# Sums over the normed rows ahead of the shift, the table load tied to the last SiLU, and the modulation tiles moved out of layer 0's last W_down piece

## The chip, the cores and the metric

The kernel runs on one core of one Trainium2 chip. Its time is device microseconds for one execution of the whole program. The chip has a matrix engine (TensorE, PE in the profile), a vector engine (VectorE, DVE), a scalar engine (ScalarE, ACT), GpSimd (POOL) and a queue engine that issues the transfers (SyncE, SP). Each engine works its own list of instructions in order.

## The reference

Two layers of a hybrid decoder on 512 rows of 1024 numbers, all in f32. Cut to what matters here:

```
c_act = silu(c)
for l in range(2):
    mod = c_act @ w_ada[l] + b_ada[l]                      # 6 x 1024 numbers
    sh1, sc1, g1, sh2, sc2, g2 = split(mod, 6)
    h = rmsnorm(x, norm1_w[l]) * (1 + sc1) + sh1
    x = x + g1 * hybrid_mixer(h)                           # W_in, attention, SSD, W_out
    h = rmsnorm(x, norm2_w[l]) * (1 + sc2) + sh2
    g, u = split(h @ w_gate_up[l], 2)                      # 1024 -> 2 x 2816
    x = x + g2 * ((silu(g) * u) @ w_down[l])               # 2816 -> 1024
```

## The kernel before

Activations lie transposed: `xT` holds 8 tiles (k = 0 to 7) of 128 features by 512 rows. Each f32 matmul operand is split into a rounded part and the rest (`hh` and `hl` for the normed rows, `hi`/`lo` for weights), and a product is three matmuls: hi with hi, hi with lo, lo with hi. ScalarE makes the rounded part (a CAST or an ACTIVATE), VectorE the rest. H0 and H1 are the two halves of 256 rows.

The **norm** (`Norm`): ScalarE squares, GpSimd adds up (`acc`; the last one on VectorE), TensorE sums over partitions (`nst`), ScalarE takes Ln and then Exp of it (`na`), VectorE finishes the reciprocal root in PSUM (`nst`). `hid` then makes, for each k, `ht` (x times gain times root, VectorE), `hh` (ScalarE, with the shift `sh` as its bias) and `hl` (VectorE).

The **FFN** (`ffn`) takes the 22 gate and up tiles one after the other. Tiles 0, 1 and each odd one are plain products; each even tile f from 2 on is done by seven smaller products (`product`), for which sums and differences of the four quarters of h (`b11`, `b12`, `b21`, `b22`, here called the block sums) are split into `t1` to `t4` at the head of the FFN, and sums of weight quarters (`sf`, `sh`, `sl`) are made per tile. W_down runs in three pieces (after tiles 5, 13 and 21); a piece loads its 8 weight tiles as `rawd`, splits them into `hid` and `lod`, and `add` puts each of the 8 outputs `dps` into `xT`. In the third piece the last three outputs are done half by half (`dps05a`, `06a`, `07a`, then `05b`, `06b`, `07b`).

The **modulation** `mod` of layer 1 is made during layer 0: `ada_some(n)` takes n of the 40 queued tiles (128x1024, `rawa`), each one transfer of 512 KB and one VectorE instruction. `rawa`, `rawd` and the weights of the mixer (`raw`, `rawr`) share three buffers of the tag `raw`, in turn.

**ScalarE's tables.** Silu needs one table set, Ln and Exp another that holds both. `exp_ln_tables()` (L249) loads that one by hand; where the active table lacks a function, the build puts a load of its own (shown at L155) before the instruction. The last FFN piece calls `exp_ln_tables()` after its last tile, and the scheduler may place it among the SiLUs in front of it:

```
if c1 == FT:
    exp_ln_tables()
```

PE's order is pinned to the program's order in the FFN; the order of ScalarE, VectorE and SP is chosen by a scheduler from its own costs when the program is built. In layer 1's mixer, `rows` makes `rps` from slabs of W_in (`hir`, and `lor` on GpSimd), then `wps` tiles of the rest are interleaved with the latents' up-projections `kvps` and `qps`, their norms (`yk`, `yy`) and transposes (`tk`, `tq`).

Of the kernel before, what the change touches and what calls it, by code (L numbers as in the profile page):

```python
# [8 lines left out]
F32 = mybir.dt.float32  # L9
# [3 lines left out]
AF = mybir.ActivationFunctionType  # L13
ALU = mybir.AluOpType
# [58 lines left out]
P = 128  # L73
S = 512
D = 1024
KT = D // P
# [9 lines left out]
FT = DFF // P  # L86
# [107 lines left out]
def trunk(ctx, tc, xin, cin, pos, eye, consts, small, wada, ws, out):  # L194
    nc = tc.nc
    ve, se, ge = Kept(tc, nc.vector), Kept(tc, nc.scalar), nc.gpsimd
# [4 lines left out]
    tp = ctx.enter_context(tc.tile_pool(name="tp", bufs=3))  # L201
# [3 lines left out]
    def T(name, shape=None, dt=F32, tag="t", pool=tp, **k):  # L205
        return pool.tile(shape or [P, S], dt, name=name, tag=tag, **k)
# [41 lines left out]
    def exp_ln_tables():  # L248
        tc.keep_in_program_order(nc.scalar.preload_act_table_set("natural_log_exp_and_others"))  # L249
# [78 lines left out]
    mods = [cp.tile([P, 48], F32, name=f"mods{l}") for l in range(L)]  # L328
# [27 lines left out]
    def ada_some(n, pool=None, pin=None):  # L356
        for _ in range(n):
            if ada_q:
                l, t = ada_q.pop(0)
                raw = None  # L360
                if pool is not None:
                    raw = pool.tile([P, 8, P], F32, name=f"rawa{l}_{t}", tag="rawa", bufs=2)
                ada1(l, t, raw, pin)
                if t % 8 == 7:
                    ada_fin(l, t - 7, t + 1)
# [51 lines left out]
            for k in ks:  # L417
                hid(self.l, self.which, h, k, rb, sl, **kw)

    def hid(l, which, h, k, rb, sl=slice(0, S), eng=None, full=None, pool=tp):  # L420
        o = 0 if which == 1 else 8
        so = (0 if which == 1 else 24) + k
        sh = mods[l][:, so:so + 1]
        hh, hl = h
        n = sl.stop - sl.start
        t = T(f"ht{l}{which}{k}_{sl.start}", [P, n] if pool is not tp else None, pool=pool, **({"bufs": 4} if pool is not tp else {}))
        ve.scalar_tensor_tensor(t[:, :n], xT[:, k, sl], gn[l][:, o + k:o + k + 1], rb[:, :n], op0=ALU.mult, op1=ALU.mult)
        if full is not None:
            se.activation(full, t[:, :n], AF.Identity, bias=sh)
        if hh is None:  # L430
            return
        se.activation(hh[:, k, sl], t[:, :n], AF.Identity, bias=sh)
        if eng is not None:
            u = T(f"hu{l}{which}{k}_{sl.start}")[:, :n]
            se.activation(u, t[:, :n], AF.Identity, bias=sh)
            return eng.tensor_tensor(hl[:, k, sl], u, hh[:, k, sl].bitcast(F32), op=ALU.subtract)
        return ve.scalar_tensor_tensor(hl[:, k, sl], t[:, :n], sh, hh[:, k, sl].bitcast(F32), op0=ALU.add, op1=ALU.subtract)

    hid_hl = (cp.tile([P, KT, S], F32R, name="hh"), cp.tile([P, KT, S], F32R, name="hl"))
# [567 lines left out]
    def ffn(l, mix, nrm2, kept):  # L1007
# [7 lines left out]
        H0, H1 = HALVES  # L1015
        HW = S // 2
        K4 = KT // 2
        hh, hl = hid_hl
# [4 lines left out]
        with tc.tile_pool(name=f"ff{l}", bufs=1) as fp:  # L1023
# [3 lines left out]
            raw, rd, sta, sf, px, py, pz, sg, p5, w, whole, gps = ({} for _ in range(12))  # L1027
# [16 lines left out]
            def tile_weights(f, i):  # L1044
                whole[f, i] = weights(raw[f][i], f"{'uw'[i]}{l}_{f}")
# [55 lines left out]
            def c12(f):  # L1101
                se.copy(sg[f][:, H1], pz[f])
                ve.tensor_tensor(sg[f][:, H1], sg[f][:, H1], px[f], op=ALU.add)
                se.activation(sg[f], sg[f], AF.Silu)

            def c22(f):
                ve.tensor_tensor(p5[f], p5[f], px[f], op=ALU.add)
# [12 lines left out]

            def gate_silu(f):
                sg[f] = T(f"sg{l}{f}")
                se.activation(sg[f], gps[0], AF.Silu)


            hp = ExitStack()
            hpool = hp.enter_context(tc.tile_pool(name=f"hf{l}", bufs=1))
            (b11, b12), (b21, b22) = ([hpool.tile([P, K4, HW], F32, name=f"b{i}{j}{l}") for j in (1, 2)] for i in (1, 2))
            full = lambda k, half: ((b11, b12), (b21, b22))[k // K4][half][:, k % K4, :]
            rb = None  # L1130
            for i, _ in enumerate(out_proj(l, mix, nrm2, H1, kept)):
                if i % KT == KT - 1:
                    i //= KT
                    if i == 0:
                        rb = nrm2.scale(H0)
                    else:
                        for k in (i - 1, i) if i == KT - 1 else (i - 1,):
                            nrm2.apply(hid_hl, rb, H0, (k,), full=full(k, 0))
                    if i in (3, 5):
                        loads(i // 2 - 1)  # L1140
                    if i >= KT - 2:
                        tile_weights(0, i - KT + 2)
# [10 lines left out]
            half(H0, range(K4))  # L1153
            rb2 = nrm2.scale(H1, tag="my")
            half(H0, range(K4, KT))
            for k in range(KT):
                nrm2.apply(hid_hl, rb2, H1, (k,), full=full(k, 1), pool=hpool)
            half(H1, range(KT))
            tile_weights(1, 0)
            ve.tensor_tensor(b11, b12, b11, op=ALU.subtract)  # L1160
            split(*ts[1], b11)
            tile_weights(1, 1)
            ve.tensor_tensor(b12, b22, b12, op=ALU.subtract)
            ve.tensor_tensor(b22, b22, b11, op=ALU.subtract)
            split(*ts[2], b22)
            ve.tensor_tensor(b21, b21, b22, op=ALU.subtract)
            split(*ts[3], b12)
            split(*ts[4], b21)
            hp.close()
# [1 line left out]
            with tc.tile_pool(name=f"ac{l}", bufs=1) as ap:  # L1171
# [5 lines left out]
                for pc, (c0, c1) in enumerate(PIECES):  # L1177
# [39 lines left out]
                    for f in range(c0, c1):  # L1217
                        if f == 0:
                            gate_silu(0)
                            unit(0, gps[1])  # L1220
                            loads(2)
                            ada_some(1)
                        elif f not in FAST and f - 1 not in FAST:
                            loads(f + 2)
                            tile_half(f, 0)
                            gate_silu(f)
                            tile_half(f, 1)
                            unit(f, gps[1])
                            sums(f + 1)
                            loads(f + 3)  # L1230
                            ada_some(1)
                        elif f in FAST:
                            g = f + 1
                            product(1, f)
                            product(2, f)
                            c11(f)
                            if late is not None:
                                product(4, late)
                                unit(late)
                            product(5, f)  # L1240
                            copy5(f)
                            tile_weights(g, 0)
                            tile_half(g, 0)
                            gate_silu(g)
                            product(6, f)
                            product(3, f)
                            c12(f)
                            tile_weights(g, 1)
                            loads(g + 2)
                            if g < c1 - 1:  # L1250
                                sums_a(g + 1)
                            else:
                                fetch(0)
                                fetch(1)
                                fetch(2)
                            tile_half(g, 1)
                            unit(g, gps[1])
                            product(7, f)
                            c22(f)
                            if g < c1 - 1:  # L1260
                                sums_b(g + 1)
                                loads(g + 3)
                            else:
                                ready(0)
                                ready(1)
                            late = f
                            if c0 == 0:
                                ada_some(3)
                    if c1 == FT:
                        exp_ln_tables()  # L1270
                    ps = {m: bank("mm", f"dps{l}{pc}_{m}") for m in (0, 1)}
                    slow = [f - c0 for f in (late, c1 - 1)]
                    ks = [k for k in range(n) if k not in slow]
# [12 lines left out]
                    for m in range(last):  # L1286
                        fetch(m + 3)
                        if m > 0:
                            ready(m + 2)
                        if m > 1:  # L1290
                            ps[m] = bank("mm", f"dps{l}{pc}_{m}")
                            down(m, FULL, range(n), ps[m])
                        add(ps[m], m, FULL)
                        ada_some(2)
                    if c1 == FT:
                        ready(KT - 1)
                tail = range(last, KT)
# [20 lines left out]
    h = None  # L1318
# [194 lines left out]
```

## Time and profile before

| | |
|---|---|
| median of 3 runs | 1312.83 us (1312.13 to 1312.91) |
| profiled execution | 1313.35 us, its span 1311.6 us |
| TensorE | 1206.6 us busy, 92% of the span; mean granted clock 0.967 |
| VectorE | 881.5 us, 67% |
| ScalarE | 625.8 us, 48% |
| GpSimd | 239.9 us, 18% |
| chain that ended last | PE 62%, DVE 16%, DMA 7%, ACT 7% |

The span is one execution from its first to its last instruction. A row of waits names the waiting engine with what it writes and its line, the releaser behind the arrow, then the total in us, how many waits, and the longest. A row of the timeline has the start, the duration in us, engine, line, operation, out and in, and in brackets the idle time ahead of it. Layer 0's FFN is at 297 to 683 us, layer 1's mixer from there to 925 us, layer 1's FFN to the end.

### The profile page before, as it was taken

Reading aid. Unit: us, or ns where it says so; the run is one execution under the profiler, and the core shown is the slowest. Engines: PE = TensorE matmul, PEld = TensorE weight load, DVE = VectorE, ACT = ScalarE, POOL = GpSimd, SP = SyncE. Lnnn points to the kernel's source line nnn. Section 1 sums busy time; section 2 is a strip of 40 time slices with the busy share of each in tenths; the row PEclk is TensorE's granted clock in tenths of the full one; section 3 lists DMA queues with packets and bytes.
Section 4 is the critical chain, followed back from the end, with each engine's and each line's share of the span. In section 5 each row is a group of like instructions: output and inputs, shape, how many; then the busy total and the mean of one; then the engine's idle time right before and its main releaser. Section 6 shows DMA issues by size and latency. Waiting matters only on the chain.

```text
span 1311.6 us, 18321 instructions
## 1 busy us (share of the span) xinstructions
PE 1206.6 (92%) x7076; PEld 1035.9 (79%) x7076; DVE 881.5 (67%) x1517; ACT 625.8 (48%) x1064; POOL 239.9 (18%) x177
## 2 busy tenths in 40 slices
PE   7879797788999999999977789988989999999998
PEld 6668674688887998899867677757978899889988
DVE  6979778879858755864565675475898456445532
ACT  4356764437532442244335977754664244324430
POOL 2651154352000000000152220446300000000000
PEclk8899998898999999999998999989999999999999
DMA  8433344463428533841343211212626343233021
GB/s 313 157 121 119 107 145 126 137 218 109 157 89 271 194 113 112 282 141 30 117 143 89 63 51 64 65 48 60 201 98 210 109 128 90 71 120 110 29 79 66
DMA packets 48727, 162.45 MB, mean 124 GB/s; under 512 B 5440, under 2 KB 8832, under 8 KB 48640
## 3 DMA queue, kind: packets, MB, share of 16 engines
q1 hardware_dynamic: 48640, 161.29, 38.6%
q8 instruction: 55, 0.90, 0.3%
q14 instruction: 32, 0.26, 0.1%
HBM read 159.14 MB, written 2.13 MB: 123 GB/s over the span
## 4 chain that ended last, share of the span: by engine, by line
PE 62%; DVE 16%; DMA 7%; ACT 7%; issue 4%; POOL 3%; DVEq 0%; ACTq 0%; POOLq 0%; SPq 0%
PE gup L139 19%; PE dps L139 11%; PE gx L139 9%; PE ops L139 5%; PE gz L139 4%; PE wps L139 4%; DMA rawa<-wada 3%; DVE rawa L155 2%; PE sc L139 2%; PE gy L139 2%; DMA raw<-ws 2%; DMA rawd<-ws 1%; PE pt L142 1%; ACT L155 1%; DVE qr L155 1%
## 5 line engine op out<-in xcount | busy, mean ns | idle before, releaser
L155 ACT CAST hid<-rawd 128x1024 fp32r<-128x1024 f32 (+1 forms) x48 | 46.6, 978 | 174.2 <-PE dps L139 62.9
L139 PE MATMUL dps<-ah,hid 128*128 128x512 f32 x304 | 120.5, 396 | 0.5 <-ACT hid L155 0.5
L139 PE MATMUL dps<-ah,lod 128*128 128x512 f32 x304 | 120.3, 396 | 0.5 <-DVE lod L155 0.5
L139 PE MATMUL dps<-al,hid 128*128 128x512 f32 x304 | 120.2, 395 | 0.0
L399 POOL TENSOR_TENSOR acc<-acc,sq 128x256 f32<-128x256 f32 x36 | 44.2, 1231 | 382.0 <-ACT sq L155 381.9
L155 DVE SCALAR_TENSOR_TENSOR rawa<-rawa,cb 128x1024 f32<-128x1024 f32 x77 | 100.9, 1320 | 11.7 <-DMA rawa<-wada 11.3
L155 ACT CAST hiu<-rawg 128x1024 fp32r<-128x1024 f32 x44 | 46.0, 1048 | 98.1 <-PE gup L139 53.6
L155 DVE TENSOR_TENSOR lou<-rawg,hiu 128x1024 fp32r<-128x1024 f32 x44 | 53.7, 1221 | 51.5 <-ACT hiu L155 51.3
L139 PE MATMUL gup<-hh,hiu 128*128 128x512 f32 (+1 forms) x208 | 79.0, 380 | 6.7 <-ACT hh L155 6.7
L155 DVE SCALAR_TENSOR_TENSOR xT<-dps,mods,xT 128x512 f32<-128x512 f32 x42 | 31.4, 749 | 71.9 <-PE dps L139 71.8
L139 PE MATMUL gup<-hh,lou 128*128 128x512 f32 (+1 forms) x208 | 78.7, 378 | 1.0 <-DVE lou L155 1.0
L139 PE MATMUL gup<-hl,hiu 128*128 128x512 f32 (+1 forms) x208 | 79.0, 380 | 0.3 <-DVE hl L155 0.2
L139 PE MATMUL gup<-hh,hiw 128*128 128x512 f32 (+1 forms) x208 | 79.0, 380 | 0.0
L139 PE MATMUL ops<-hh,hi 128*128 128x256 f32 x256 | 75.3, 294 | 3.9 <-DVE xT L155 1.7
L139 PE MATMUL gup<-hh,low 128*128 128x512 f32 (+1 forms) x208 | 78.7, 379 | 0.0
L139 PE MATMUL gup<-hl,hiw 128*128 128x512 f32 (+1 forms) x208 | 78.4, 377 | 0.0
L155 DVE TENSOR_TENSOR lod<-rawd,hid 128x1024 fp32r<-128x1024 f32 (+1 forms) x48 | 54.2, 1133 | 35.1 <-ACT hid L155 34.5
L139 PE MATMUL ops<-hl,hi 128*128 128x256 f32 x256 | 73.1, 286 | 1.0 <-POOL hl L443 1.0
L139 PE MATMUL ops<-hh,lo 128*128 128x256 f32 x256 | 73.1, 286 | 0.8 <-POOL lo L291 0.8
L139 PE MATMUL wps<-hh,hi 128*128 128x512 f32 x168 | 70.7, 421 | 2.4 <-DVE xbc L155 2.4
L139 PEld LDWEIGHTS dps<-ah,lod 128*128 128x128 f32 x304 | 57.1, 188 | 15.2 <-DVE lod L155 1.4
L139 PEld LDWEIGHTS dps<-ah,hid 128*128 128x128 f32 x304 | 57.1, 188 | 14.4 <-ACT hid L155 1.3
(438 smaller groups left out, 3696.9 us busy)
## 6 DMA issues: line engine op xcount, KB each, us to landing
rawg<-ws SPq DMA_DIRECT2D x88, 512.0 KB, 3.8
rawa<-wada SPq DMA_DIRECT2D x80, 512.0 KB, 4.3
raw<-ws SPq DMA_DIRECT2D x49, 512.0 KB, 3.7
rawd<-ws SPq DMA_DIRECT2D x32, 512.0 KB, 3.7
raws<-wada SPq DMA_DIRECT2D x16, 512.0 KB, 5.0
rawd<-ws SPq DMA_DIRECT2D x16, 384.0 KB, 3.6
ar<-ard SPq DMA_DIRECT2D x8, 512.0 KB, 3.9
rawk<-ws SPq DMA_DIRECT2D x8, 404.0 KB, 5.4
```

The source lines that it names most:

```text
L139: self._put(self.tc.nc.tensor.matmul(out, lhsT, rhs, **kw), 4 * n if rhs.dtype == F32 else n)
L142: self._put(self.tc.nc.tensor.transpose(out, in_, eye), 0.116)
L155: i = f(*args, **kw)
L399: (ve if last else eng or ge).tensor_tensor(self.acc[:, sl], self.acc[:, sl], sq, op=ALU.add)
```

## The change

It has three parts, all in `ffn` and `hid`.

1. The block sums are taken from `ht`, the rows before the shift. `hid` no longer writes an f32 copy of the shifted rows on ScalarE; `ht` is written straight into the tile `tt`, and the shift enters the sums through `sh` or `dsh` (a difference of shifts) as a per-partition scalar. Three of the four sums of 128x1024 become four instructions of 128x256 each.
2. `exp_ln_tables()` in the last piece waits for the last two SiLUs.
3. In the second and third piece `ada_some(1)` is called after each even tile, and `ada_some(2)` no longer in the W_down part of the third piece.

```
-    def hid(l, which, h, k, rb, sl=slice(0, S), eng=None, full=None, pool=tp):
+    def hid(l, which, h, k, rb, sl=slice(0, S), eng=None, full=None):
...
-        t = T(f"ht{l}{which}{k}_{sl.start}", [P, n] if pool is not tp else None, pool=pool, **({"bufs": 4} if pool is not tp else {}))
+        t = T(f"ht{l}{which}{k}_{sl.start}") if full is None else full[:, k, sl]
         ve.scalar_tensor_tensor(t[:, :n], xT[:, k, sl], gn[l][:, o + k:o + k + 1], rb[:, :n], op0=ALU.mult, op1=ALU.mult)
-        if full is not None:
-            se.activation(full, t[:, :n], AF.Identity, bias=sh)
...
+            tt = hpool.tile([P, KT, S], F32, name=f"tt{l}")
+            sh = mods[l][:, 24:32]
+            dsh = hpool.tile([P, K4], F32, name=f"dsh{l}")
+            ve.tensor_tensor(dsh, sh[:, K4:KT], sh[:, 0:K4], op=ALU.subtract)
...
+            b11, b12, b21, b22 = (tt[:, ks, sl] for ks in (slice(0, K4), slice(K4, KT)) for sl in (H0, H1))
             ve.tensor_tensor(b11, b12, b11, op=ALU.subtract)
             split(*ts[1], b11)
             tile_weights(1, 1)
-            ve.tensor_tensor(b12, b22, b12, op=ALU.subtract)
-            ve.tensor_tensor(b22, b22, b11, op=ALU.subtract)
+            for k in range(K4):
+                ve.scalar_tensor_tensor(b12[:, k], b22[:, k], dsh[:, k:k + 1], b12[:, k], op0=ALU.add, op1=ALU.subtract)
+            for k in range(K4):
+                ve.scalar_tensor_tensor(b22[:, k], b22[:, k], sh[:, K4 + k:K4 + k + 1], b11[:, k], op0=ALU.add, op1=ALU.subtract)
             split(*ts[2], b22)
-            ve.tensor_tensor(b21, b21, b22, op=ALU.subtract)
+            for k in range(K4):
+                ve.scalar_tensor_tensor(b21[:, k], b21[:, k], sh[:, K4 + k:K4 + k + 1], b22[:, k], op0=ALU.add, op1=ALU.subtract)
...
-                            gate_silu(g)
+                            i1 = gate_silu(g)
...
-                            c12(f)
+                            i2 = c12(f)
...
-                            if c0 == 0:
-                                ada_some(3)
+                            ada_some(3 if c0 == 0 else 1)
                     if c1 == FT:
-                        exp_ln_tables()
+                        with tc.issue_after(i1.ins), tc.issue_after(i2.ins):
+                            exp_ln_tables()
...
-                        ada_some(2)
+                        if c1 < FT:
+                            ada_some(2)
```

ScalarE at the end of layer 0's last piece: `sg` are the gate values of tiles 21 and 20, `hid_2_1` and `hid_2_2` the rounded W_down tiles. Before:

```order
L155 CAST hid_2_1_5703<-rawd_2_1_5653 128x1024
L155 ACTIVATE sg_5618<-gup_5593 128x512
L249 ACT_TABLE_LOAD
L155 COPY sg_5556<-gz_20_5574 128x256
L155 ACT_TABLE_LOAD
L155 ACTIVATE sg_5556<-sg_5556 128x512
L155 CAST hid_2_2_5743<-rawd_2_2_5655 128x1024
```

Now:

```order
L155 CAST hid_2_1_5700<-rawd_2_1_5650 128x1024
L155 ACTIVATE sg_5615<-gup_5590 128x512
L155 COPY sg_5553<-gz_20_5571 128x256
L155 ACTIVATE sg_5553<-sg_5553 128x512
L249 ACT_TABLE_LOAD
L155 CAST hid_2_2_5745<-rawd_2_2_5652 128x1024
```

The load of the Ln and Exp set stood between the last two SiLUs, so a second load fetched Silu's set again; now it stands behind both. ScalarE's whole list has 36 table loads before and 12 now: 22 of those that are gone stood one by one before the Ln and Exp instructions of layer 1's first norm and mixer.

VectorE in layer 0's FFN head, from the last split of the block sums (`t4l`) to the low parts of tile 3's weights (`lou_3`, `low_3`). Before:

```order
L155 TENSOR_TENSOR t4l_2641<-b_2647,t4h_2640 128x1024
L155 TENSOR_TENSOR lou_2_3218<-rawg_2_0_3151,hiu_2_3217 128x1024
L155 TENSOR_TENSOR al_3144<-sg_3146,ah_3143 128x512
L155 SCALAR_TENSOR_TENSOR rawa_46_3155,mods_92<-rawa_46_3155,cb 128x1024
L155 TENSOR_TENSOR sg_3187<-sg_3187,gup_3189 128x512
L155 TENSOR_TENSOR sf_2_3_3232<-rawg_2_0_3151,rawg_2_1_3153 128x512
L155 TENSOR_TENSOR lou_3_3292<-rawg_3_0_3158,hiu_3_3291 128x1024
L155 TENSOR_TENSOR al_3144<-sg_3187,ah_3143 128x512
L155 TENSOR_TENSOR sl_2_3_3234<-sf_2_3_3232,sh_2_3_3233 128x1024
L155 SCALAR_TENSOR_TENSOR rawa_47_3243,mods_92<-rawa_47_3243,cb 128x1024
L155 TENSOR_TENSOR sg_3273<-sg_3273,gx_2_3247 128x256
L155 TENSOR_TENSOR mods_92<-mods_92,sm_72 128x8
```

Now:

```order
L155 TENSOR_TENSOR t4l_2641<-tt_2645,t4h_2640 128x1024
L155 TENSOR_TENSOR lou_2_3194<-rawg_2_0_3127,hiu_2_3193 128x1024
L155 TENSOR_TENSOR al_3120<-sg_3122,ah_3119 128x512
L155 SCALAR_TENSOR_TENSOR rawa_46_3131,mods_92<-rawa_46_3131,cb 128x1024
L155 TENSOR_TENSOR sg_3163<-sg_3163,gup_3165 128x512
L155 TENSOR_TENSOR sl_2_3_3210<-sf_2_3_3208,sh_2_3_3209 128x1024
L155 TENSOR_TENSOR al_3120<-sg_3163,ah_3119 128x512
L155 SCALAR_TENSOR_TENSOR rawa_47_3219,mods_92<-rawa_47_3219,cb 128x1024
L155 TENSOR_TENSOR sg_3249<-sg_3249,gx_2_3223 128x256
L155 TENSOR_TENSOR mods_92<-mods_92,sm_72 128x8
L155 TENSOR_TENSOR lou_3_3268<-rawg_3_0_3134,hiu_3_3267 128x1024
L155 TENSOR_TENSOR low_3_3326<-rawg_3_1_3136,hiw_3_3325 128x1024
```

`lou_3` has moved from the seventh place behind `t4l` to the eleventh; it now stands behind a split, a modulation tile and a sum that waits for tile 2's products. The first `sf_2_3` has left this stretch: it runs ahead of the block sums. Layer 1's head has the same move.

VectorE in layer 0's last W_down piece, from the rest of W_down tile 3 (`lod_2_3`) on; `xT` is the update of the rows, `rawa` a modulation tile of layer 1. Before:

```order
L155 TENSOR_TENSOR lod_2_4_5810<-rawd_2_4_5788,hid_2_4_5809 128x1024
L155 SCALAR_TENSOR_TENSOR rawa_34_5801,mods_93<-rawa_34_5801,cb 128x1024
L155 SCALAR_TENSOR_TENSOR rawa_35_5804,mods_93<-rawa_35_5804,cb 128x1024
L155 SCALAR_TENSOR_TENSOR xT<-dps_3_5857,mods_92,xT 128x512
L155 TENSOR_TENSOR lod_2_5_5854<-rawd_2_5_5807,hid_2_5_5853 128x1024
L155 SCALAR_TENSOR_TENSOR rawa_36_5845,mods_93<-rawa_36_5845,cb 128x1024
```

Now:

```order
L155 TENSOR_TENSOR lod_2_4_5800<-rawd_2_4_5784,hid_2_4_5799 128x1024
L155 SCALAR_TENSOR_TENSOR xT<-dps_2_5803,mods_92,xT 128x512
L155 TENSOR_TENSOR lod_2_5_5838<-rawd_2_5_5797,hid_2_5_5837 128x1024
L155 SCALAR_TENSOR_TENSOR xT<-dps_3_5841,mods_92,xT 128x512
L155 TENSOR_TENSOR lod_2_6_5876<-rawd_2_6_5835,hid_2_6_5875 128x1024
```

The eight tiles that stood here are gone from this stretch. Layer 1's tiles 16 to 19 and 36 to 39 now follow the even gate and up tiles of the second and third piece, one each, and the second piece's W_down takes tiles 20 to 35 where it took 16 to 31.

## Rows read from the trace of the kernel before

**Rows 1.** Busy time by stretch; the first line names the columns.

```profile
core 0: us, PE busy (x) PEld busy (x) DVE busy (x) ACT busy (x) POOL busy (x), PEclk, DMA share, GB/s
297.00:346.00 49.00, 45.70 (x301) 42.69 (x300) 47.85 (x73) 34.12 (x59) 6.42 (x5) 0.93 0.37 110
440.00:520.00 80.00, 80.00 (x464) 70.50 (x463) 45.57 (x67) 30.03 (x42) 0.00 (x0) 1.00 0.32 103
722.00:793.00 71.00, 58.36 (x286) 48.09 (x284) 50.43 (x128) 61.33 (x98) 18.72 (x16) 0.95 0.18 53
1262.00:1300.00 38.00, 38.00 (x210) 32.69 (x209) 13.65 (x19) 5.78 (x6) 0.00 (x0) 1.00 0.26 84
```

**Rows 2.** Waits of TensorE, 640 to 700 us.

```profile
PE rps L139 <- DVE ht L155: 8.3, 1, 8.3
...
PE dps07a L139 <- ACT hid L155: 2.3, 1, 2.3
PE dps07a L139 <- DVE lod L155: 0.8, 1, 0.8
PE dps06a L139 <- DVE lod L155: 0.7, 1, 0.7
```

**Rows 3.** Timeline of TensorE, 669 to 686 us.

```profile
669.42 0.42 PE L139 MATMUL dps07a<-ah,hid 128*128 128x256 f32 x1
...
672.42 0.40 PE L139 MATMUL dps07a<-ah,lod 128*128 128x256 f32 x1
...
673.37 0.28 PE L139 MATMUL dps05b<-ah,hid 128*128 128x256 f32 x1
...
676.10 0.28 PE L139 MATMUL dps05b<-ah,lod 128*128 128x256 f32 x1
...
685.99 0.93 PE L139 MATMUL nst<-acc,ones 128*128 128x256 f32 x2 [3.50 <-DVE acc L155]
```

**Rows 4.** Waits of TensorE, 722 to 793 us.

```profile
PE kvps L139 <- ACT lh L155: 4.1, 1, 4.1
PE tk L142 <- ACT kT L155: 3.1, 2, 1.7
PE tq L142 <- DVE qr L155: 2.8, 2, 1.9
PE tq L142 <- ACT cd L155: 2.3, 1, 2.3
```

**Rows 5.** Table loads of ScalarE: count, busy us, mean ns, idle us before.

```profile
L155 ACT ACT_TABLE_LOAD x29 | 37.2, 1283 | 5.5 <-DVE xbc L155 1.9 <-DVE lv L155 1.9 <-DVE hl L155 1.3
```

**Rows 6.** Timeline of VectorE in layer 0's FFN head, 317 to 345 us.

```profile
317.39 1.65 DVE L155 SCALAR_TENSOR_TENSOR ht<-xT,gn,nst 128x256 f32<-128x256 f32 x4
...
340.11 1.22 DVE L155 TENSOR_TENSOR lou<-rawg,hiu 128x1024 fp32r<-128x1024 f32 x1
...
344.46 0.16 DVE L155 TENSOR_TENSOR mods<-mods,sm 128x8 f32<-128x8 f32 x1
```

**Rows 7.** Timeline of VectorE, 682 to 685 us.

```profile
682.23 2.10 DVE L155 SCALAR_TENSOR_TENSOR nst<-na 128x256 f32<-128x256 f32 x1
684.24 0.47 DVE L155 SCALAR_TENSOR_TENSOR xT<-dps07b,mods,xT 128x256 f32<-128x256 f32 x1
```

**Rows 8.** Timeline of GpSimd, 681 to 684 us.

```profile
681.89 2.15 POOL L299 TENSOR_TENSOR lor<-rawr,hir 128x848 fp32r<-128x848 f32 x1 [1.79 <-ACT hir L155]
```

**Rows 9.** Waits of TensorE in layer 0's mixer, 95 to 165 us.

```profile
PE tq L142 <- DVE qr L155: 3.5, 1, 3.5
...
PE kvps L139 <- ACT lh L155: 2.2, 1, 2.2
```

**Rows 10.** Timeline of ScalarE, 723 to 725 us.

```profile
723.09 0.30 ACT L155 ACTIVATE ly<-lv,eps 128x12 f32<-128x12 f32 x1
...
724.71 0.21 ACT L155 ACTIVATE ly<-ly 128x12 f32<-128x12 f32 x1
```

**Rows 11.** Timeline of TensorE, the first low-part matmul of tile 3.

```profile
343.07 0.39 PE L139 MATMUL gup<-hh,lou 128*128 128x512 f32 x1
```

More of the change, by code (lines that the diff above doesn't have):

```diff
@@ L425, in hid @@
         n = sl.stop - sl.start
-        t = T(f"ht{l}{which}{k}_{sl.start}", [P, n] if pool is not tp else None, pool=pool, **({"bufs": 4} if pool is not tp else {}))
+        t = T(f"ht{l}{which}{k}_{sl.start}") if full is None else full[:, k, sl]
         ve.scalar_tensor_tensor(t[:, :n], xT[:, k, sl], gn[l][:, o + k:o + k + 1], rb[:, :n], op0=ALU.mult, op1=ALU.mult)
-        if full is not None:
-            se.activation(full, t[:, :n], AF.Identity, bias=sh)
-        if hh is None:
-            return
         se.activation(hh[:, k, sl], t[:, :n], AF.Identity, bias=sh)
@@ L1103, in c12 @@
                 ve.tensor_tensor(sg[f][:, H1], sg[f][:, H1], px[f], op=ALU.add)
-                se.activation(sg[f], sg[f], AF.Silu)
+                return se.activation(sg[f], sg[f], AF.Silu)
             def c22(f):
@@ L1122, in gate_silu @@
                 sg[f] = T(f"sg{l}{f}")
-                se.activation(sg[f], gps[0], AF.Silu)
+                return se.activation(sg[f], gps[0], AF.Silu)
             hp = ExitStack()
             hpool = hp.enter_context(tc.tile_pool(name=f"hf{l}", bufs=1))
-            (b11, b12), (b21, b22) = ([hpool.tile([P, K4, HW], F32, name=f"b{i}{j}{l}") for j in (1, 2)] for i in (1, 2))
-            full = lambda k, half: ((b11, b12), (b21, b22))[k // K4][half][:, k % K4, :]
+            tt = hpool.tile([P, KT, S], F32, name=f"tt{l}")
+            sh = mods[l][:, 24:32]
+            dsh = hpool.tile([P, K4], F32, name=f"dsh{l}")
+            ve.tensor_tensor(dsh, sh[:, K4:KT], sh[:, 0:K4], op=ALU.subtract)
             rb = None
@@ L1137, in ffn @@
                         for k in (i - 1, i) if i == KT - 1 else (i - 1,):
-                            nrm2.apply(hid_hl, rb, H0, (k,), full=full(k, 0))
+                            nrm2.apply(hid_hl, rb, H0, (k,), full=tt)
                     if i in (3, 5):
@@ L1155, in ffn @@
             half(H0, range(K4, KT))
-            for k in range(KT):
-                nrm2.apply(hid_hl, rb2, H1, (k,), full=full(k, 1), pool=hpool)
+            nrm2.apply(hid_hl, rb2, H1, full=tt)
             half(H1, range(KT))
             tile_weights(1, 0)
+            b11, b12, b21, b22 = (tt[:, ks, sl] for ks in (slice(0, K4), slice(K4, KT)) for sl in (H0, H1))
             ve.tensor_tensor(b11, b12, b11, op=ALU.subtract)
```

## The prediction

> **What bounds the kernel now.** I read the busy time by stretch first, then TensorE's waits stretch by stretch, then the timelines around the longest of them. In most of the FFN TensorE is the bound: 440 to 520 us has it busy 80.00 of 80 us at a granted clock of 1.00, with VectorE at 45.57 [rows 1]. An edit there costs nothing unless it makes TensorE wait. The change touches three places where it does wait or nearly does.
>
> The first is layer 0's last W_down piece and the norm behind it. TensorE waits 2.3, 0.8 and 0.7 us for the halves of W_down weights (`hid`, `lod`), then 3.50 us for the sum of squares, then 8.3 us for `ht` [rows 2, 3]. The second is the front of layer 1's mixer, 722 to 793 us: TensorE is busy 58.36 of 71 us, ScalarE 61.33, the most of all engines [rows 1], and TensorE's waits name ScalarE and what VectorE makes behind it [rows 4]. ScalarE has 29 table loads of 1283 ns that the build put there [rows 5]; 22 of them stand in layer 1's first norm and mixer, one before nearly every Ln and every Exp. The third is the FFN's head: at 297 to 346 us VectorE is busy 47.85 of 49 us [rows 1]. There nearly any VectorE work that is added is late by its whole length.
>
> **Modulation tiles out of layer 0's last W_down.** Eight transfers and eight VectorE instructions leave a stretch in which they held the three `raw` buffers and so the W_down loads. Layer 1's last W_down is the model, since it has no such tiles: TensorE is busy 38.00 of 38 us there at clock 1.00 [rows 1]. So all of 2.3 + 0.8 + 0.7 = 3.8 us goes. The stops also left the granted clock at its lower level: 15 matmuls of `dps07a` start 0.214 us apart (669.42 to 672.42), 24 of `dps05b` 0.119 us apart (673.37 to 676.10) [rows 3]. Some 16 slow ones by 0.095 is 1.5 us. Together 5.3 us; bounds 3.8 and 5.3.
>
> The eight tiles land between gate and up tiles, where VectorE is idle 43% of the time [rows 1]; each is one instruction of 128x1024 (about 1.2 us, as a split of that shape [rows 6]). Behind it on VectorE wait the first sum of the running even tile, which TensorE needs only after a whole odd half tile, and a late product for W_down. On SP's queue the modulation transfers now stand ahead of `rawd`, each in a buffer free since the piece before; `rawd_1_0` follows once its tile is consumed, two even tiles before its use. I cost this at nothing; without that cover it is 8 x 1.2 = 9.6 us.
>
> **Table loads, layer 1's first norm.** The two loads before Ln and Exp of the first half are on the path: Exp, `na`, `nst`, and on VectorE behind `nst` the update `xT<-dps07b`, which starts at 684.24 [rows 7], although TensorE was done with its matmuls when its wait began, at 685.99 - 3.50 = 682.49 [rows 3]. With `nst` 2.57 us earlier that update starts right behind the matmuls, so 684.24 - 682.5 = 1.7 us goes. The next two loads, 2.57 us, stand in the second half's chain, which decides the 8.3 us wait [rows 2]; after them VectorE's own list is next (`ht` and `hl` of both halves). I take 2.6. Sum 4.3; bounds 3.0 and 5.9, since the list could also move closer together.
>
> GpSimd matters here. `nst` took 2.10 us while GpSimd's `lor` ran (2.15 us, begun 0.34 us earlier); the `xT` update after it took 0.47 [rows 7, 8]. The Trainium skill (SBUF — State Buffer, "Who interferes with whom") says that VectorE with two SBUF inputs and GpSimd share a port pair as an exclusive lock, held for a whole instruction. The rows agree, and by that rule the three slabs would each block one VectorE instruction wherever it now falls, so the blocks would stay and this term with them; had the rule not held, 1.6 us more would be won.
>
> **Table loads, the mixer's front.** Before `kvps` two loads lie in a row of dependent steps, 2.57 us of a wait of 4.1 [rows 4]; layer 0 has the same wait, without such loads, at 2.2 [rows 9]. So 1.9 to 2.6; I take 2.2. The `tk` waits (3.1 us, ScalarE's own lateness [rows 4]) do not exist in layer 0: 3.1, bounds 1.5 and 3.1. The `tq` waits, 2.8 + 2.3 [rows 4], hang on `yy`, with two loads before each; but layer 0 has a `tq` wait of 3.5 for `qr` [rows 9] without any load, so VectorE is close behind: bounds 0 and 5.1, I take the middle, 2.6. Sum 7.9. What VectorE does next decides what is late then. The clock in this stretch is 0.95 [rows 1]: a tenth of 71 us at the lower level costs 3.5 us of TensorE's work; fewer stops give back part, I take 1.0, bounds 0 and 3.5.
>
> The Trainium skill (ScalarE: Activation LUTs, "What ACT_TABLE_LOAD costs") puts a switch of sets at 1283 ns plus a drain of about 1380. The load agrees with its row [rows 5]. The drain does not show: Ln ends at 723.39, Exp starts at 724.71 with a load between, 1.32 us in all [rows 10]. By the page these terms would double; I keep the rows' figure.
>
> **Block sums in the two FFN heads.** Sixteen f32 copies per layer leave ScalarE. TensorE's restart after the norm gains nothing, since ScalarE's list now has a 128x1024 cast (`sh_2_3`) just ahead of the first `hh`: 0, half a microsecond either way. On VectorE three sums of 1.22 us [rows 6] become twelve short ones; four of that shape take 1.65 [rows 6], so 4.95 for 3.66, 1.29 us more per layer. That alone would hide in the gaps behind the head. But the order counts: `lou_3` finished at 341.3 [rows 6] and TensorE asked for it at 343.07 [rows 11]; now everything up to the `mods` row (done 344.6 [rows 6]) stands ahead of it, and 1.29 us more. The head's 1.15 us of idle [rows 1] can take up little. So `lou_3` ends near 345.5 and TensorE waits 2.4 us on tile 3, in either layer: 4.8 us. Bounds: 1.5 per layer if the idle time is used to the full; 3.9 if TensorE's clock falls behind the stop as it did before `dps07a`, 1.5 us more.
>
> **Sum.** Gains 5.3 + 4.3 + 7.9 + 1.0 = 18.5 us, losses 4.8: net 13.7. The profiled execution took 1313.35, 0.5 above the median of the runs. 1313.35 - 13.7 = 1299.65; as a median about 1299.
>
> **Rivals.**
> *All waits go.* ScalarE was the only cause in the front: 5.3 + 5.9 + (2.6 + 3.1 + 5.1) + 3.5 = 25.5, less 3.0 in the heads, 22.5: as a median 1290.5. For it: ScalarE's load in that stretch; against it: layer 0's `tq` wait.
> *VectorE holds the front.* Only the shares on a plain chain come back: 5.3 + 1.7 + 2.2 = 9.2, less 4.8: 4.4 won, 1308.5. For it: VectorE busy 50.43 of 71 [rows 1] with every norm's chain running through it.
> *Slower: VectorE holds both places.* The twelve short sums depend on each other; if each costs its full latency and not its share of a run of four, about 0.16 us more, `lou_3` is 2.4 + 1.9 = 4.3 late, and the clock falls behind it (1.5): 5.8 per layer, 11.6. If the front, held by the same engine, gives back only 5.3 + 1.7 = 7.0, that is 4.6 lost: 1317.5. It turns slower from 3.5 us per head on. For it: the heads have 1.15 us of idle VectorE time [rows 1]; against it: TensorE's waits of the front name ScalarE first [rows 4].
> *The loads stay.* The built lists show them gone; no chance of its own.
>
> **How the numbers follow.** Forecast 0.52, all waits go 0.22, VectorE holds the front 0.17, slower 0.09. The range takes both neighbours in: 1289 to 1310, for 8 in 10. About 0.2% (2.6 us) is what a measurement of this kernel can tell from no change. The first two cases are faster throughout, of the third 0.12 (0.05 within 0.2%), the last is slower: faster 0.86, within 0.05, slower 0.09.
>
> **What would show it.** ScalarE's group of table loads falls from 29 to 5. No `hid` or `lod` wait of TensorE in the last W_down of layer 0, clock 1.00 there. The `nst` wait falls to about 1.8 us, `rps` to under 6, `kvps` to about 2, `tk` to nothing. A new wait of TensorE for `lou`, 2.4 us in each head, at the second tile pair. Were `tq` waits longer than 2.5 us in all, VectorE holds more than I give it; were there no `lou` wait, the heads are mis-sized. I am wrong altogether if TensorE's idle time in 676 to 793 us stays where it is.

## The result, and the profile after

The changed kernel takes 1297.81 us (median; 1292.08 to 1299.60), the kernel before 1312.87 in the same runs: a ratio of 0.9873, 95% interval 0.9838 to 0.9909. That is 15 to 17 us less; the forecast was 1299. One single execution of all runs, of the kernel with the table load alone, took 1479.5 us at a granted clock of 0.75; it is left out of the medians and ratios below.

First the table loads of ScalarE. Group of instructions, count, busy us, mean ns, idle us before:

```profile
L155 ACT ACT_TABLE_LOAD x5 | 6.4, 1283 | 1.9 <-DVE xbc L155 1.9
```

24 of the 29 loads of [rows 5] are gone. What one of them cost in a chain is seen at the first Ln and Exp of the latents' norm, ScalarE's timeline after:

```profile
714.62 0.30 ACT L155 ACTIVATE ly<-lv,eps 128x12 f32<-128x12 f32 x1 [1.90 <-DVE lv L155]
714.96 0.21 ACT L155 ACTIVATE ly<-ly 128x12 f32<-128x12 f32 x1
```

Exp now starts 0.34 us after Ln; before it was 1.62 [rows 10]. The difference, 1.28 us, is the load and nothing more. The Trainium skill (ScalarE: Activation LUTs, "What ACT_TABLE_LOAD costs") adds a drain of about 1380 ns to each switch to another set; these two pairs of starts show none.

Now the places. Busy time of the engines in the stretches that answer to [rows 1]: the first FFN head, the last W_down of layer 0, and the mixer's front, from the restart of `rps` to the last `tq`. The last row, of the kernel before, is the same front there (696.28 to 792.10 us):

```profile
core 0: us, PE busy (x) PEld busy (x) DVE busy (x) ACT busy (x) POOL busy (x), PEclk, DMA share, GB/s
297.00:346.00 49.00, 42.60 (x279) 39.03 (x278) 46.69 (x77) 28.34 (x42) 4.75 (x4) 0.97 0.40 120
640.00:676.00 36.00, 36.00 (x223) 32.13 (x222) 14.57 (x19) 13.02 (x24) 13.22 (x13) 1.00 0.24 71
688.56:771.50 82.94, 80.07 (x399) 70.03 (x400) 65.56 (x158) 50.75 (x112) 25.02 (x19) 0.97 0.26 75
```
```profile
696.28:792.10 95.82, 83.19 (x398) 71.28 (x399) 63.93 (x158) 74.01 (x130) 24.63 (x19) 0.95 0.23 65
```

The front is 12.9 us shorter for the same matmuls: 9.8 us less idle time of TensorE (95.82 - 83.19 before, 82.94 - 80.07 now) and 3.1 us less busy time, at a granted clock of 0.97 for 0.95. ScalarE went from 74.01 to 50.75 us. The W_down has TensorE busy throughout at clock 1.00. In the head TensorE has lost: 42.60 us of 49, where it had 45.70.

TensorE's waits in the changed kernel; engine, what it writes, releaser, total us, count, longest. First 640 to 702 us, against [rows 2, 3], then 702 to 774, against [rows 4], then layer 0's and layer 1's head:

```profile
PE rps L139 <- DVE ht L155: 8.0, 1, 8.0
PE nst L139 <- DVE acc L155: 1.8, 1, 1.8
...
PE tq L142 <- ACT cd L155: 1.5, 1, 1.5
PE kvps L139 <- ACT lh L155: 1.2, 1, 1.2
...
PE gup L139 <- ACT hh L155: 4.1, 1, 4.1
PE gup L139 <- DVE lou L155: 2.0, 1, 2.0
...
PE gup L139 <- ACT hh L155: 3.8, 1, 3.8
PE gup L139 <- DVE lou L155: 1.9, 1, 1.9
```

The waits for `hid`, `lod`, `tk` and `qr` are gone, those for `kvps` and `cd` small. The wait before `rps` has hardly moved. In the heads the `lou` wait is new, and the wait for the first `hh` is longer than before (3.3 and 3.5 us there). VectorE at the new `lou` wait of layer 0:

```profile
340.54 1.22 DVE L155 SCALAR_TENSOR_TENSOR rawa<-rawa,cb 128x1024 f32<-128x1024 f32 x1
341.69 0.08 DVE L155 DVE_READ_ACCUMULATOR rawa<-rawa,cb 128x1 f32 x1
341.69 0.42 DVE L155 TENSOR_TENSOR sg<-sg,gx 128x256 f32<-128x256 f32 x1
342.02 0.16 DVE L155 TENSOR_TENSOR mods<-mods,sm 128x8 f32<-128x8 f32 x1
342.10 1.22 DVE L155 TENSOR_TENSOR lou<-rawg,hiu 128x1024 fp32r<-128x1024 f32 x1
```

`lou_3` starts behind the modulation tile, the product and `mods`, without a gap, and TensorE restarts 1.27 us after its start, at 343.37 [against rows 6, 11].

### The profile page after: what moved, and what is told of

Read it like the earlier page. It is cut to its first block, busy times and chain, and to the rows that moved or that the text cites. A ratio compares the mean times of both kernels' runs of the same rounds, so it can differ in the third digit from the quotient of the medians.

```text
span 1297.4 us, 18251 instructions
## 1 busy us (share of the span) xinstructions
PE 1203.5 (93%) x7076; PEld 1032.0 (80%) x7076; DVE 880.8 (68%) x1537; ACT 583.3 (45%) x1008; POOL 233.6 (18%) x177
## 5 line engine op out<-in xcount | busy, mean ns | idle before, releaser
L399 POOL TENSOR_TENSOR acc<-acc,sq 128x256 f32<-128x256 f32 x36 | 37.4, 1044 | 388.7 <-ACT sq L155 388.7
L155 DVE SCALAR_TENSOR_TENSOR rawa<-rawa,cb 128x1024 f32<-128x1024 f32 x77 | 98.0, 1279 | 9.9 <-DMA rawa<-wada 9.7
```

What stands on the lines that cost most here:

```text
L155: i = f(*args, **kw)
L399: (ve if last else eng or ge).tensor_tensor(self.acc[:, sl], self.acc[:, sl], sq, op=ALU.add)
```

## The experiments

Each part alone came first and two of them together, then four kernels on what the traces left unexplained. Every ratio is to the kernel before, measured beside it; a figure in us behind it is that ratio, or its interval, times the median of the kernel before. "Between the same matmuls" means: the traces hold the same 7076 matmuls in the same order (some lack one record), so the time between the same two starts can be compared (the places are in the table further down).

**The table load alone (e_table).** `tc.issue_after` makes what stands in it wait for the instruction named; `i1` and `i2` are the last two SiLUs.

```
                    if c1 == FT:
-                       exp_ln_tables()
+                       with tc.issue_after(i1.ins), tc.issue_after(i2.ins):
+                           exp_ln_tables()
```

> The kernel before with the second part alone (the load of the Ln/Exp table waits for the last two SiLUs; 12 table loads are left of 36). Theory A, each part works in its own place and the parts add: the wait for `nst` falls to about 1.8 us (-1.7), the restart of `rps` comes about 0.8 us sooner, and the mixer's front (`kvps`, `tk`, `tq`) gains 12 to 13: 1296 to 1299 us, 14 to 16 under the kernel before; the last W_down keeps its waits and its clock, the heads keep theirs. Rival B, the front's gain in the changed kernel came from all three parts together (an undisturbed VectorE ahead of it): this part alone gives 8 to 10 us, 1303 to 1305, with part of the `kvps` and `tq` waits left.

Measured: 1294.04 us, ratio 0.9872 (0.9849 to 0.9895), 16.8 us less. Theory A, a little more gain than its range. The trace is of a second run.

> The second part alone once more, for its trace. Theory A, the parts add: `nst` at the norm waits 1.8 us, `rps` 7.5 to 8.0, the front has no wait for `tk` over 0.5 us and no more than 2 us of `kvps` in layer 1; the last W_down keeps waits of 3 to 4 us. Rival B, some of the front's gain belongs to the other parts: 2 us or more of `kvps`, `tk` and `tq` waits are there that the kernel without the first part doesn't have.

Measured: ratio 0.9858 (0.9835 to 0.9881). Waits of TensorE at 630 to 690, then 690 to 790 us:

```profile
PE rps L139 <- DVE ht L155: 7.7, 1, 7.7
PE dps07a L139 <- ACT hid L155: 2.3, 1, 2.3
PE nst L139 <- DVE acc L155: 1.8, 1, 1.8
PE dps07a L139 <- DVE lod L155: 0.8, 1, 0.8
...
PE kvps L139 <- ACT lh L155: 1.9, 1, 1.9
PE tq L142 <- ACT cd L155: 1.5, 1, 1.5
```

The whole gain of the front and the 1.7 us at `nst` belong to the table load: between the same matmuls the front is 13.4 us shorter here, 12.9 in the changed kernel. The W_down keeps its waits. Theory A holds, rival B falls.

**The modulation tiles alone (e_ada).**

```
-                           if c0 == 0:
-                               ada_some(3)
+                           ada_some(3 if c0 == 0 else 1)
...
-                       ada_some(2)
+                       if c1 < FT:
+                           ada_some(2)
```

> The kernel before with the third part alone (no modulation tile in layer 0's last W_down, one after each even tile of the second and third piece). Theory A: the waits on `hid` and `lod` in that W_down go and its clock rises to 1.00, 5 to 6 us of it, and nothing else changes: 1306.5 to 1308. Rival B: what is saved in the W_down is taken back by the table loads, which still stand there (the last matmul group comes sooner, the norm's chain with its loads doesn't): the wait for `nst` grows and 0 to 3 us are left, 1310 to 1313.

Measured: 1305.40 us, ratio 0.9951 (0.9933 to 0.9969), 6.4 us less, a little more than Theory A's range. No wait for `hid` or `lod` stands in the last W_down; `nst` still waits 3.5 us and `rps` 8.5. Theory A: nothing is taken back by the loads behind.

**The block sums alone (e_sums).** All of the diff in `hid` and ahead of `hp.close()`, and no more.

> The kernel before with the first part alone (the sums from the rows ahead of the shift). Theory A: each FFN head has a `lou` wait of 2.0 us and a longer wait for the first `hh` (4.1 for 3.25 in layer 0, 3.8 for 3.5 in layer 1), layer 1's head a lower clock besides: 5 to 8 us slower, 1318 to 1321. Rival B: the head's loss in the changed kernel is the clock's and the run's, and the ScalarE time saved gives something back elsewhere: within 2 us of the kernel before, 1311 to 1315.

Measured: 1321.08 us, ratio 1.0073 (1.0050 to 1.0095), 9.6 us slower (6.6 to 12.5). Theory A in kind, above its range. Waits in layer 0's and layer 1's head:

```profile
PE gup L139 <- ACT hh L155: 4.1, 1, 4.1
PE gup L139 <- DVE lou L155: 2.0, 1, 2.0
...
PE gup L139 <- ACT hh L155: 4.8, 1, 4.8
PE gup L139 <- DVE lou L155: 1.9, 1, 1.9
```

That is 6.0 us more than before's two `hh` waits (3.3 and 3.5). Between the same matmuls the heads are 2.7 and 4.6 us longer, 7.3 in all, inside the interval. The trace is of the fastest of the six executions; the 2.3 us up to the 9.6 stay open.

**The change without its block sums (e_nosums).** The kernel before with the two diffs above together.

> The changed kernel without its first part (the f32 copies and the sums as before; the table load and the modulation tiles as changed). Theory A: the two heads lose nothing, all else is as in the changed kernel: 5 to 8 us under it, 1290 to 1293. Rival B: the sums cost nothing by themselves: 1296 to 1299, as the changed kernel.

Measured: 1288.24 us, ratio 0.9821 (0.9799 to 0.9844), 23 us under the kernel before. Theory A in kind; the time is 2 us under its range. The parts add: -16.8 - 6.4 is -23.2; with the 9.6 of the sums it is -13.6, and the changed kernel, run again beside the later kernels, gave 0.9890 (-14.4; 0.9873 is -16.7).

**The changed kernel once more (e_after2).**

> The changed kernel again, word for word, as the measure for the run beside it: 0.985 to 0.991 of the kernel before by either theory.

Measured: 1295.63 us, ratio 0.9890 (0.9865 to 0.9915).

**Why the wait for `rps` did not fall (e_uh).** In the changed kernel's trace ScalarE reaches the fifth `hh` only at 685.99, behind the cast `uh`, which waits for a transfer. SP's queue and its waits, GpSimd, ScalarE, VectorE:

```profile
677.28 4.80 SPq L307 DMA_DIRECT2D raw<-ws  x2
...
SPq L307 <- POOL lor L299: 6.9, 2, 4.1
```
```profile
679.57 2.16 POOL L299 TENSOR_TENSOR lor<-rawr,hir 128x848 fp32r<-128x848 f32 x1
```
```profile
682.12 0.47 ACT L155 ACTIVATE na<-nst,eps 128x256 f32<-128x256 f32 x1 [1.31 <-DVE hl L155]
...
685.14 0.93 ACT L155 ACTIVATE uh<-raw,sm 128x768 fp32r<-128x768 f32 x1 [1.85 <-DMA raw<-ws]
685.99 0.89 ACT L155 ACTIVATE hh<-ht,mods 128x256 fp32r<-128x256 f32 x2
```
```profile
680.20 1.81 DVE L155 SCALAR_TENSOR_TENSOR hl<-ht,mods,hh 128x256 fp32r<-128x256 f32 x1
686.51 0.48 DVE L155 SCALAR_TENSOR_TENSOR hl<-ht,mods,hh 128x256 fp32r<-128x256 f32 x1 [1.74 <-ACT hh L155]
```

Both `raw` transfers wait for a `lor` of GpSimd to end and give its buffer back. The first starts at 677.28, as the second `lor` ends (675.24 to 677.26); the second starts at about 681.75 (677.28 + 4.80, less its own 0.33), as the third ends, and lands at 685.1. In the kernel before the same pair spans 684.06 to 689.05; its second transfer took 3.1 us from its start at 688.7 and landed at about 691.8, and `uh` ran at 692.88 behind two table loads. No more than 1.1 us could be won there. The experiment puts `uh` behind the last `hh`, in the kernel without block sums:

```
+            with tc.issue_after(last_hh[-1].ins) if l == 1 else nullcontext():
                 se.activation(hi, raw[:, :n], AF.Identity, scale=scale)
```

> The changed kernel without its first part, and the two casts `uh` of W_up's first blocks in layer 1's mixer issued behind the last `hh` of the norm. In the runs so far `uh` stands on ScalarE ahead of the fifth `hh` and waits 1.6 to 1.9 us there for its transfer, which SP issues 4.5 us after the last W_down group. Theory A, that wait took the place of the two table loads in the restart of `rps`: the wait before `rps` falls from 7.4 to between 5.0 and 6.0, the rest stays, 1.5 to 2.5 us less than without the first part: ratio to the kernel before 0.980 to 0.981. Rival B, VectorE's own list (the `ht` of the second half, `nst`, the `hl`) or GpSimd's port sets the restart: the wait stays at 7.0 to 8.0 and the time too, ratio 0.982. Rival C: the casts come too late behind `hh`, `kvps` or `qps` wait for them, and the time rises by 1 to 4 us.

Measured: 1286.56 us, ratio 0.9807 (0.9792 to 0.9823); waits at 655 to 690 us:

```profile
PE rps L139 <- DVE ht L155: 6.1, 1, 6.1
PE nst L139 <- DVE acc L155: 1.8, 1, 1.8
```

TensorE from `nst` to the restart of `rps`, in the changed kernel and then in this one:

```profile
679.02 0.70 PE L139 MATMUL nst<-acc,ones 128*128 128x256 f32 x2 [1.84 <-DVE acc L155]
688.56 0.72 PE L139 MATMUL rps<-hir,hh 128*128 128x424 f32 x1 [7.97 <-DVE ht L155]
...
675.03 0.70 PE L139 MATMUL nst<-acc,ones 128*128 128x256 f32 x2 [1.85 <-DVE acc L155]
682.76 0.72 PE L139 MATMUL rps<-hir,hh 128*128 128x424 f32 x1 [6.14 <-DVE ht L155]
```

The wait fell by 1.3 us, from 7.4, a little less than A said; the time fell by about as much, which the two intervals don't tell apart. So `uh` was what came late after the loads. From `nst` to the restart it is 10.29 us before (685.99 to 696.28), 9.54 in the changed kernel, 9.28 in e_nosums and 7.73 here: only with `uh` out of the way, its own 0.93 us included, does this place gain the 2.6 us of the forecast. Rival C shows in part, with `kvps` at 1.7 us for 1.2; but the last `tq` wait, 1.5, is gone. It has the lowest ratio of the study, in an interval that overlaps those of e_nosums and e_best.

Of the 6.1 us left, VectorE's `hl` of 1.81 us (0.48 elsewhere) beside GpSimd's `lor` is one step: ScalarE's `na` of the second half waits 1.31 us for it. The Trainium skill (SBUF — State Buffer, "Who interferes with whom") has a VectorE instruction with two inputs in SBUF and a GpSimd one that reads SBUF share a port, locked for a whole instruction; by that each of the three slabs can block VectorE once. In the changed kernel's trace the third does (`hl`), the first a little (`na` took 0.90 us at 673.38, as `lor` ended at 673.99, for its usual 0.42); the second, 675.24 to 677.26, falls into VectorE's wait for `dps07b`.

**Whether `lou_3`'s place is the heads' loss (e_late).** The changed kernel, with tile 2's second sums recorded later:

```
-                           sums(f + 1)
-                           loads(f + 3)
+                           sums_a(f + 1)
...
                            tile_weights(g, 0)
+                           if f == 2:
+                               sums_b(f)
+                               loads(f + 2)
```

> The changed kernel with the second half of tile 2's block sums (`sums_b(2)`, and the load behind it) recorded behind `tile_weights(3, 0)`: on VectorE `lou_3` now stands ahead of `sl_2_3`, `sg(gx_2)` and, in layer 0, one modulation tile. All else of the change stays. Theory A, the place of `lou_3` in VectorE's list costs the 2.0 us in each head: those two waits fall under 0.5 us, 3 to 4.5 us less than the changed kernel. Rival B, VectorE is late there as a whole: the wait passes on to the next tiles (`low_3`, `sl_2_3`) and the time is that of the changed kernel within 1 us.

Measured: 1290.96 us, ratio 0.9840 (0.9824 to 0.9857) against 0.9890 beside it: 4.7 to 6.6 us less by medians and ratios, Theory A and more. No `lou` wait is left in either head, and none comes in its place. The place in the list was the cause. Between the same matmuls the heads are 1.7 and 3.6 us shorter than in the changed kernel, more than the waits of 2.0 and 1.9; layer 1's trace of the changed kernel shows where that comes from. TensorE there:

```profile
961.36 0.40 PE L139 MATMUL gup<-hl,hiu 128*128 128x512 f32 x1
963.68 0.74 PE L139 MATMUL gup<-hh,lou 128*128 128x512 f32 x1 [1.92 <-DVE lou L155]
964.22 0.63 PE L139 MATMUL gup<-hh,hiu 128*128 128x512 f32 x1
964.65 0.63 PE L139 MATMUL gup<-hl,hiu 128*128 128x512 f32 x1
...
967.20 0.40 PE L139 MATMUL gup<-hl,hiu 128*128 128x512 f32 x1
967.44 0.40 PE L139 MATMUL gup<-hh,lou 128*128 128x512 f32 x1
```

After the stop the matmuls start 0.43 us apart, nearly twice the 0.23 of later ones, until 967.20: 3.52 us for eight, where 8 x 0.23 is 1.84, so some 1.7 us more. The granted clock of 956 to 969 us is 0.87 in the changed kernel and 1.00 in this one.

**Why the first `hh` waits longer (e_norm).** In the changed kernel ScalarE and VectorE work on tile 2's sums (`vh`, `sh`, `vl`, `sl`) between the steps of the norm. This kernel is e_late with those issued behind the last `hh`:

```
+                           with tc.issue_after(ffn_hh[-1].ins) if f == 1 else nullcontext():
                                sums_a(f + 1)
```

> The kernel with `lou_3` ahead of `sl_2_3`, and tile 2's first sums (`vh`, `sh` on ScalarE, `vl`, `sl` on VectorE) issued behind the last `hh` of the FFN's norm, where they stood inside the norm's chain. On VectorE they now stand ahead of `lou_3`. Theory A, these casts and subtractions in the norm's chain made the wait for the first `hh` 4.0 to 4.2 us: it falls to 2.2 to 3.2 us in each head (1.1 us for `vh` and `sl` apiece), and since VectorE has the same work to do before `lou_3`, a `lou` wait of 1 to 3 us comes back: the time is within 3 us of the kernel with `lou_3` ahead, 0.982 to 0.987 of the kernel before. Rival B, the chain is bound by its own instructions: `hh` waits 3.8 to 4.2 us as before, and the `lou` wait comes on top: 0.987 to 0.990.

Measured: 1293.56 us, ratio 0.9858 (0.9823 to 0.9892). Layer 0's and layer 1's head:

```profile
PE gup L139 <- DVE lou L155: 2.0, 1, 2.0
PE gup L139 <- ACT hh L155: 1.9, 1, 1.9
...
PE gup L139 <- ACT hh L155: 2.0, 1, 2.0
PE gup L139 <- DVE lou L155: 1.9, 1, 1.9
```

Theory A: the `hh` waits fell from 4.0 and 4.2 to 1.9 and 2.0, and the `lou` waits came back, 2.0 and 1.9. A wait of 2 us was moved, not removed. That VectorE has that much to do in the head whichever way it is ordered fits this, and is argued, not shown.

**All of it together (e_best).** The fastest kernel with both re-orderings of tile 2's sums.

> The changed kernel without its first part, with `uh` behind the norm's last `hh`, tile 2's second sums behind `tile_weights(3, 0)` and its first sums behind the FFN norm's last `hh`. Theory A: the `hh` waits fall from 3.3 to about 2 us each, and `lou_3`, behind the moved sums, waits 0.5 to 2.5 us: between 1283 and 1288 us, no clear gain over the kernel with `uh` alone (0.981). Rival B, VectorE has slack behind the head: no `lou` wait, 1.5 to 3 us less, ratio 0.978 to 0.979.

Measured: 1288.85 us, ratio 0.9819 (0.9788 to 0.9850): no gain over 0.9807. `hh` waits 2.7 us and `lou` 1.2 in layer 0, 2.7 and 1.1 in layer 1. Theory A, with the `hh` waits longer than the 2 it gave them and the time 1 us above its range.

## Why the prediction was right, and which terms were not

The forecast was 1299.0 and the range 1289 to 1310; the time is 1297.81. The mechanism is the one forecast, place by place, but for one step. That the sum came within 1.2 us is luck: four of its terms are off, and the errors cancel. The start of the same matmul in the trace before and in the changed kernel's, us:

| place | forecast | before | now | difference |
|---|---|---|---|---|
| last W_down | -5.3 | 640.04 to 682.21 | 640.88 to 676.90 | -6.15 |
| `nst` | -1.7 | 682.21 to 685.99 | 676.90 to 679.02 | -1.66 |
| `rps` | -2.6 | 685.99 to 696.28 | 679.02 to 688.56 | -0.75 |
| front, with its clock | -8.9 | 696.28 to 792.23 | 688.56 to 771.58 | -12.93 |
| layer 0's head | +2.4 | 297.02 to 350.10 | 294.46 to 350.53 | +2.99 |
| layer 1's head | +2.4 | 925.10 to 1000.21 | 905.53 to 986.40 | +5.77 |

The front gave 4.0 us more than forecast, the heads cost 4.0 more, W_down gave 0.9 more and `rps` 1.8 less. The rows come to -12.7; the other stretches of the two traces differ by -1.1 in all. The second trace of the changed kernel (e_after2) has each row within 0.4 us.

- *W_down, -5.3.* Alone it measured -6.4 (4.1 to 8.8 less), and 6.15 between the same matmuls. The waits of 3.8 us went as forecast; that leaves 2.3 for the lower clock, for which I had 1.5. The eight tiles cost little where they went: TensorE's waits from 345 to 640 us are 2.9 us in all, 2.4 before.
- *`nst`, -1.7.* The wait is 1.8 us, as named, and the table load alone shows it.
- *`rps`, -2.6.* This step failed. "The next two loads, 2.57 us, stand in the second half's chain" is true, but with them gone something else comes last: `uh`'s transfer landed only 1.1 us before `uh` ran, and `uh` stands ahead of the `hh`. The wait fell from 8.3 to 8.0, and the place gained about 0.8 us, under my lower bound of 1.3. I had looked for what is next on VectorE, and it was a transfer that waits for GpSimd's buffer. With `uh` out of the way the place gains 2.6 and the wait is 6.1, near the "under 6" that I had named.
- *The mixer's front, -7.9, and its clock, -1.0.* Too small: 12.9 in all, 9.8 of waits and 3.1 of busy time at the higher clock. The clock is the largest miss, near its upper bound of 3.5. Of the waits it is `tq`: I took the middle of 0 and 5.1, since VectorE might be close behind; only 1.5 us of it is left, so 3.6 went, against 2.6. `kvps` gave 2.9 for 2.2 (2.1 in the second trace), `tk` 3.1 as said. VectorE was busy 65.56 us of a front of 82.94, and no wait of TensorE there names it now: the rival by which it holds the front is refuted, the one by which all waits go there was nearly right.
- *The heads, +4.8.* Too small: 8.8. The twelve short sums are sized right: the seven of them that stand together start 0.40 us apart (2.85 us in all at 328.11), so twelve take 4.8 for the 4.95 I had. The `lou` waits are 2.0 and 1.9 us for 2.4, at the instruction named, and moving `lou_3` removes them. But I had set the wait for `hh` at "0, half a microsecond either way"; it grew by 0.8 and 0.3 us, since tile 2's casts slipped into the norm's chain with the copies gone. In layer 0 these two make the whole loss. In layer 1 the rest is mostly the clock: the matmuls behind the `hh` wait start 0.21 us apart, later 0.12, for 6.4 us (936.98 to 943.38) and not 3.7 (955.73 to 959.46 before), and those behind the `lou` stop were slow for another 3.5 us, which layer 0's were not, though the stops are alike. I had a clock loss only in the upper bound. Alone the sums cost 9.6 us (6.6 to 12.5), double the term.
- *The slower rival* needed gains of 7.0 us, with nothing from the front, and heads that lose 5.8 each. The gains came to 21.5. Layer 1's head did lose 5.8, by the clock; its cause, short sums that each cost their full latency, did not show.

The first part of the change is a loss in itself, 9.6 us alone. Without it the other two give 0.9821. With `lou_3` put right the kernel with it stands at 0.9840; the two intervals overlap, but in its trace the heads are still 3.5 us longer than before.

## What to carry to other kernels

Before a stall is booked as gone, look at what the next instruction on the same engine waits for, transfers too: its data may land little earlier than the stall ended. Work taken off an engine with idle time (ScalarE in the head) at the price of longer work on the full one (VectorE) cost more than its length here, 8.8 us for some 2.6, because the order behind it shifted and the clock fell behind the stops. A scheduler's table loads are worth counting in the built list: one preload that stands a few instructions too early cost 24 loads and 17 us here.

## What the hardware showed beyond the forecast

Two stops of TensorE of the same length, 2.0 and 1.9 us, had different ends: behind the one in layer 0 the clock was granted in full, behind the one in layer 1 matmuls ran at nearly half the rate for 3.5 us (963.68 to 967.20). The second trace of the changed kernel has the same pair (slow from 962.69 to 966.22). The layer doesn't decide it: with the sums alone (e_sums) and in e_norm the stop in layer 1 is 1.9 us again, and the matmuls behind it start 0.23 us apart. Nor does an earlier dip of the clock by itself: the changed kernel's layer 1 had been at 0.66 from 935 to 945 us and at 1.00 from 945 to 955, ahead of the stop, and that of e_sums at 0.71 from 950 to 960 and at 1.00 from 965 to 980. What sets the difference was not tried.
